# Mixing first in four groups of 512, then the feed-forward in three groups of 704: a hybrid decoder layer on one core

## The chip, the core and the metric

The kernel runs on one core of one Trainium2 chip. The metric is the device time of one execution in microseconds (us), the median of several runs. The engines are named as in the profile: PE (TensorE, matmuls; PEld its weight loads), DVE (VectorE), ACT (ScalarE), POOL (GpSimd), and SP (SyncE), whose queue issues nearly all DMAs.

## The reference

One decoder layer over a prompt of 2048 tokens and a sample of 8 x 8 = 64 tokens that share all weights: model width 1024, feed-forward width 4096. Cut to what matters:

```python
proj = rmsnorm(x, norm_mix_w) @ w_in            # 1024 -> 4096 columns
# 4 retention heads: q, k (rotary), v, gate; 4 HGRN2 heads: q, f, v, gate; all 128 wide
o_r = (head_rmsnorm(chunk_gla(rq, rk, rv, log_gamma)) * silu(rg))
o_h = (head_rmsnorm(chunk_gla(hq, 1 - f, hi, log(f))) * silu(hg))
x = x + concatenate([o_r, o_h]) @ w_out         # 1024 -> 1024, the residual
x = x + square(relu(rmsnorm(x, norm_ffn_w) @ w_up)) @ w_down
y = rmsnorm(x, final_norm_w)                    # for prompt and sample; the final states of the heads are outputs too
```

`chunk_gla` is a causal linear recurrence S_t = diag(g_t) S_(t-1) + k_t^T v_t, o_t = q_t S_t. The prompt starts from zero states, each of the eight samples from its own given state.

## The kernel before

Activations lie transposed, with features on the 128 partitions and tokens along the columns. A float32 product is made by three fp32r matmuls: each operand is cut in a rounded part `hi` and the rest `lo`, and hi·hi, hi·lo and lo·hi are added up in PSUM. A weight unit is 128x1024. It is loaded to a tile `raw`, ACT casts it to `hi` (L277), and DVE or POOL subtracts to make `lo` (`second_part`, L292); that subtraction is called a cut here.

The 2112 tokens go through in three groups: 512 prompt tokens; 64 sample and 768 prompt tokens (832); 768 prompt tokens. A group wider than 512 columns is worked in two pieces of half its width (416, 384), since one PSUM bank holds 512 numbers per partition. Each group runs through everything before the next one begins:

- `mix`: for each of 4 head pairs (one retention, one HGRN2 head) the input projection by `proj` (L352), the values (`values`, L728, always 256 columns), the recurrence in chunks of 128 (`mixer`), and the head norm with its gate (`gate`: L368 Ln, L369 Exp, L1161 multiply).
- `out_proj`: the residual. It stays in SBUF for the feed-forward of that group.
- the feed-forward. Group 0 does it plainly (`ffn_first`: `up_first`, `down_first`). Groups 1 and 2 do it by seven products in place of eight (`ffn`: `up_quad` for the first of eight up sets, `up` for the others, `down` for eight sets in four pairs). A pair of down sets is called an octet: 7 products times 2 sets, 14 weight units of 24 matmuls.

Seven products need sums of weight quarters, S1 to S4, and sums of activation quarters, T1 to T4 (`block_sum`, L1382; the cut of each operand is in `halve`, L1371 and L1375). The weight sums are made once, by DVE, beside the work of groups 0 and 1 (`plan_sums`, L1324), and written to DRAM (`sums`). Groups 1 and 2 read them back like any weight. The products' PSUM results are added by DVE (L1516 in `up`, L1589 in `down`). The hi and lo parts of the input projection's and residual's weights made in group 0 are also written to DRAM and read back by groups 1 and 2 (`kept`, entries "p" of the stream).

The order of the work is set in the code: `plan_stream` lists the weight units in order of use, `weight(i)` loads and prepares units up to two ahead, and side work is put on an agenda (`later(n, fn)`: after n more calls of `tick`, one for each product step). The program of each engine runs in the resulting order. `fetch` (L241) keeps some DMAs of the SP queue in program order.

The lines that cut and choose the engine for a weight:

```python
            if pool or j < 4:
                self.second_part(j, self.nc.gpsimd if pool else self.nc.vector)
            else:
                self.later(4, self.second_part, j, self.nc.vector)
...
        self.stream += [entry(name, ("d", o, v), W_DQ0 + 4 * (2 * o + v), not end and (2 * k + v) % 5 in (1, 3))
                        for v in range(2)]
```

Of the kernel before, what the change touches and what calls it, by code (L numbers as in the profile page):

```python
# [28 lines left out]
SLAB = 832  # L29
NSLAB = 42  # L30
NLD = 6
# [5 lines left out]
GROUPS = ((0, 0, 512), (NS, 512, 768), (0, 1280, 768))  # L37
NT = NS + SEQ
WT = 1024
N_IN, N_OUT, N_UP, N_DN = 32, 8, 32, 32  # L40
W_OUT0 = N_IN
W_UP0 = W_OUT0 + N_OUT
W_DN0 = W_UP0 + N_UP
NQ = FF // (4 * P)
NO = NQ // 2

W_UQ0 = W_DN0 + N_DN
W_DQ0 = W_UQ0 + N_UP
NW = W_DQ0 + N_DN

N_MADE = 4

# [10 lines left out]
PLACE = {name: q for q, name in QUARTER.items()}  # L63
# [17 lines left out]
N_ORDER = (0, 1, 4, 5, 2, 3, 6, 7)  # L81

# [63 lines left out]
def in_blocks():  # L146
    for p in range(H):
        if p:
            yield from ((7, p - 1), (3, p - 1))
        yield from ((5, p), (4, p), (0, p), (1, p), ("v", p))  # L150
    yield from ((7, H - 1), (3, H - 1))


def lay_out_weights(w_in, w_out, w_up, w_down):
    w = np.empty((NW, P, WT), np.float32)
    wi = w_in.reshape(KB, P, 8, H, DK)
    i = 0
    for part, p in in_blocks():
        if part != "v":
            w[i] = wi[:, :, part, p].transpose(1, 0, 2).reshape(P, WT)  # L160
            i += 1
            continue
# [6 lines left out]
    for ps in (range(0, H - 1), range(H - 1, H)):  # L169
        bl = [wo[kind, p, :, n] for n in N_ORDER for p in ps for kind in (1, 0)]  # L170
        for j in range(0, len(bl), 8):
            w[i] = np.stack(bl[j:j + 8], 1).reshape(P, WT)
            i += 1
    wu = w_up.reshape(KB, P, FF // P, P)
    for f in range(FF // P):
        w[i] = wu[:, :, f].transpose(1, 0, 2).reshape(P, WT)
        i += 1
    wd = w_down.reshape(8, 4, P, 4, 256)
    for f in range(8):
        for n in range(4):  # L180
            w[i] = wd[f, :, :, n].transpose(1, 0, 2).reshape(P, WT)
            i += 1
# [25 lines left out]
class Kernel:  # L208
# [12 lines left out]
    def tick(self):  # L221
        self.now += 1
        while self.agenda and self.agenda[0][0] <= self.now:
            _, _, fn, a = heapq.heappop(self.agenda)
            fn(*a)
        self.n_ticks += 1
        while self.side and self.side[0][0] <= self.n_ticks:
            self.side.popleft()[1]()
# [8 lines left out]
    def get(self, dt=F32):  # L237
        return self.sl.tile([P, SLAB], dt, tag="slab", name="slab")
# [6 lines left out]
    def load(self):  # L245
        return self.ld.tile([P, SLAB], F32, tag="ld", name="ld")

# [4 lines left out]
    def weight(self, i):  # L252
        n = len(self.stream)
        while self.w_next < min(i + 1 + self.ahead, n):
            j = self.w_next
            e = self.stream[j]
            if e[0] == "p":

                self.wts[j] = tuple(self.wp.tile([P, WT], F32R, tag=tag, name=tag) for tag in ("hi", "lo"))
                for part, kept in zip(self.wts[j], self.kept[e[1]]):  # L260
                    self.nc.sync.dma_start(part.bitcast(F32), kept)
                self.w_next += 1
                self.w_load = max(self.w_load, j + 1)
                continue
            while self.w_load <= j or j >= self.n_first and self.w_load <= j + 2 and self.w_load < n:
                if self.stream[self.w_load][0] == "p":
                    break
                k, later = self.w_load, self.w_load >= self.n_first
                raw = self.raws[k] = self.wp.tile([P, WT], F32, tag="sum" if later and k % 3 else "raw", name="raw",
                                                  bufs=4 if later and k % 3 else 2)  # L270
                e = self.stream[k]
                self.fetch(raw, self.sums[e[1]] if e[0] == "s" else self.I["w"][e[1]])
                self.w_load += 1
            raw = self.raws.pop(j)
            hi = self.wp.tile([P, WT], F32R, tag="hi", name="hi")
            lo = self.wp.tile([P, WT], F32R, tag="lo", name="lo")
            self.nc.scalar.copy(hi, raw)  # L277
            self.wts[j] = (hi, lo)
            self.second[j] = raw
            pool = len(self.stream[j]) > 2 and self.stream[j][2]  # L280
            if pool or j < 4:
                self.second_part(j, self.nc.gpsimd if pool else self.nc.vector)
            else:
                self.later(4, self.second_part, j, self.nc.vector)
            self.w_next += 1
        self.second_part(i, self.nc.vector)
        return self.wts[i]

    def second_part(self, j, eng):
        if j in self.second:  # L290
            hi, lo = self.wts[j]
            eng.tensor_tensor(out=lo, in0=self.second.pop(j), in1=hi.bitcast(F32), op=ALU.subtract)  # L292

    def plan_stream(self):

        self.stream = [("w", j) for j in range(W_UP0)]
        up = [[("w", W_UP0 + 4 * t + i) for i in range(4)] for t in range(NQ)]
        dn = [[("w", W_DN0 + 4 * t + i) for i in range(4)] for t in range(NQ)]
        self.stream += up[0]
        for t in range(NQ):  # L300
            self.stream += (up[t + 1] if t < NQ - 1 else []) + dn[t]
        self.n_first = len(self.stream)

        def entry(name, key, i0, pool):
            return ("s", key + (name,), pool) if name[0] == "S" else ("w", i0 + A_PLACE[name], pool)

        for g in range(1, len(GROUPS)):
            self.stream += [("p" if j >= N_MADE else "w", j) for j in range(W_UP0)]
            self.stream += [("w", W_UQ0 + i, i % 2) for i in range(4)]
            for t in range(1, NQ):  # L310
                self.stream += [entry(name, ("u", t), W_UQ0 + 4 * t, name in ("A12", "S1", "S4")) for name, _ in PRODUCTS]
            for o in range(NO):
                for k, (name, *_) in enumerate(LAST_OCTET if o == NO - 1 else OCTET):
                    end = g == len(GROUPS) - 1 and o == NO - 1 and k > 4
                    self.stream += [entry(name, ("d", o, v), W_DQ0 + 4 * (2 * o + v), not end and (2 * k + v) % 5 in (1, 3))
                                    for v in range(2)]

    def next_weight(self):
        i = self.w_use
        self.w_use += 1  # L320
        r = self.weight(i)
        if N_MADE <= i < W_UP0:
            self.kept[i] = [self.dp.tile([P, WT], F32, name=f"w{i}{part}") for part in ("hi", "lo")]
            for part, kept in zip(r, self.kept[i]):
                self.nc.sync.dma_start(kept, part.bitcast(F32))
        self.wts.pop(i - 4, None)
        return r

    def take(self, n):

        out = []
        for _ in range(n):
            if not self.blocks:
                hi, lo = self.next_weight()
# [1469 lines left out]
```

## Time and profile before

| | us |
|---|---|
| median of 3 runs (lowest to highest) | 2559.78 (2559.78 to 2560.04) |
| span of the profiled execution | 2557.8 |
| its PE busy / DVE / ACT / POOL | 2527.3 / 1702.4 / 1172.3 / 704.8 |
| DMA moved in it | 443.13 MB, 173 GB/s in the mean |

The profiled execution's own time is taken as its span and the 2.0 us by which the median lies above it. A "busy" engine is one with an instruction in flight; matmuls are pipelined, so the time of one is best read from how many fit in a stretch. In 40 slices the granted TensorE clock reads 9 (nine tenths or more) throughout. By the widths of the matmuls (512, 416 and 384 columns) the three groups take about 630, 1010 and 920 us.

### The profile page before, as it was taken

How to read it: one execution, taken by the hardware profiler on the slowest of the kernel's cores; microseconds unless marked ns; L12 is line 12 of the kernel's file. 1: busy time of each engine (PE TensorE's matmuls, PEld its weight loads, DVE VectorE, ACT ScalarE, POOL GpSimd, SP SyncE). 2: the span in 40 equal slices, each digit the busy share in tenths (PEclk: the TensorE clock that was granted, in tenths of full speed). 3: DMA queues.
4: the chain of work that ended last, by engine and by line, in shares of the span. 5: the costliest groups of instructions: out<-in, count | busy, mean ns of one | idle time of the engine just before them, and what ended most of it. 6: DMA issues, size and time to landing. Idle time of an engine off the chain costs nothing. (4 is left out here: it accounts for less than half of the span.)

```text
span 2557.8 us, 37262 instructions
## 1 busy us (share of the span) xinstructions
PE 2527.3 (99%) x14681; PEld 2398.5 (94%) x14681; DVE 1702.4 (67%) x2165; ACT 1172.3 (46%) x1591; POOL 704.8 (28%) x453
## 2 busy tenths in 40 slices
PE   8999999999999999999999999999999999999997
PEld 7888888888999999999999999999999999999997
DVE  6777775556667667664656978775456465559886
ACT  6776532325444444344434544544445264344443
POOL 4333241111324243101222322243134012223222
PEclk9999999999999999999999999999999999999999
DMA  7666854563264564634457545342223325565552
GB/s 265 219 220 223 294 197 172 190 215 125 94 231 152 198 205 173 230 126 165 166 171 258 191 173 170 129 165 93 94 100 112 120 91 179 176 226 186 176 179 83
DMA packets 147391, 443.13 MB, mean 173 GB/s; under 512 B 15120, under 2 KB 37392, under 8 KB 147216
## 3 DMA queue, kind: packets, MB, share of 16 engines
q1 hardware_dynamic: 147072, 440.73, 49.8%
q8 instruction: 116, 1.90, 0.3%
q14 instruction: 59, 0.48, 0.1%
q10 hardware_dynamic: 144, 0.02, 0.0%
HBM read 331.11 MB, written 108.79 MB: 172 GB/s over the span
## 5 line engine op out<-in xcount | busy, mean ns | idle before, releaser
L352 PE MATMUL pj<-slab,hi 128*128 128x416 f32 (+2 forms) x2844 | 739.3, 363 | 7.4 <-ACT hi L277 6.3
L277 ACT CAST hi<-raw 128x1024 fp32r<-128x1024 f32 x330 | 347.7, 1054 | 673.4 <-PE pu L1176 191.5
L352 PEld LDWEIGHTS pj<-slab,hi 128*128 128x128 f32 x2844 | 513.0, 189 | 38.7 <-ACT hi L277 6.3
L292 POOL TENSOR_TENSOR lo<-raw,hi 128x1024 fp32r<-128x1024 f32 x92 | 248.0, 2695 | 849.6 <-ACT hi L277 788.9
L1176 PE MATMUL pd<-slab,hi 128*128 128x416 f32 (+1 forms) x1792 | 469.4, 342 | 5.1 <-DVE slab L1619 3.1
L292 DVE TENSOR_TENSOR lo<-raw,hi 128x1024 fp32r<-128x1024 f32 x238 | 302.0, 1269 | 199.1 <-ACT hi L277 198.6
L352 PE MATMUL pj<-slab,lo 128*128 128x416 f32 (+2 forms) x1422 | 433.6, 363 | 0.0
L1176 PE MATMUL pu<-slab,hi 128*128 128x416 f32 (+1 forms) x1600 | 408.3, 342 | 0.0
L1176 PEld LDWEIGHTS pd<-slab,hi 128*128 128x128 f32 x1792 | 329.6, 188 | 8.7 <-DVE slab L1619 3.7
L1176 PE MATMUL pd<-slab,lo 128*128 128x416 f32 (+1 forms) x896 | 307.8, 344 | 0.0
L1176 PEld LDWEIGHTS pu<-slab,hi 128*128 128x128 f32 x1600 | 294.0, 188 | 1.5
L352 PEld LDWEIGHTS pj<-slab,lo 128*128 128x128 f32 x1422 | 259.5, 188 | 15.4 <-DVE lo L292 0.8
L1176 PE MATMUL pu<-slab,lo 128*128 128x416 f32 (+1 forms) x800 | 264.2, 343 | 0.0
L352 PE MATMUL mm<-slab,hi 128*128 128x512 f32 x740 | 229.6, 390 | 0.0
L728 PE MATMUL pjv<-hi,slab 128*128 128x256 f32 x1088 | 212.4, 287 | 1.3 <-ACT slab L738 1.3
L1375 DVE TENSOR_TENSOR slab<-slab 128x832 fp32r<-128x832 f32 (+1 forms) x144 | 163.0, 1149 | 36.9 <-ACT slab L1371 17.4
L728 PEld LDWEIGHTS pjv<-hi,slab 128*128 128x128 f32 x1088 | 174.3, 190 | 3.7 <-ACT slab L738 2.2
L1371 ACT CAST slab<-slab 128x832 fp32r<-128x832 f32 (+1 forms) x144 | 122.4, 862 | 116.2 <-DVE slab L1382 83.2
L1176 PEld LDWEIGHTS pd<-slab,lo 128*128 128x128 f32 x896 | 168.1, 188 | 0.5
L352 PEld LDWEIGHTS mm<-slab,hi 128*128 128x128 f32 x740 | 138.5, 188 | 29.2 <-ACT slab L1206 0.4
L728 PE MATMUL pjv<-lo,slab 128*128 128x256 f32 x544 | 153.8, 283 | 0.0
L1176 PEld LDWEIGHTS pu<-slab,lo 128*128 128x128 f32 x800 | 149.7, 188 | 0.5
(214 smaller groups left out, 3685.8 us busy)
## 6 DMA issues: line engine op xcount, KB each, us to landing
raw<-w SPq DMA_DIRECT2D x270, 512.0 KB, 4.2
u<-ld SPq DMA_DIRECT2D x32, 416.0 KB, 4.5
slab<-u SPq DMA_DIRECT2D x32, 416.0 KB, 5.6
u<-ld SPq DMA_DIRECT2D x32, 384.0 KB, 4.5
slab<-u SPq DMA_DIRECT2D x32, 384.0 KB, 5.7
ld<-x SPq DMA_DIRECT2D x16, 416.0 KB, 6.1
ld<-x SPq DMA_DIRECT2D x16, 384.0 KB, 4.1
raw<-su1S SPq DMA_DIRECT2D x8, 512.0 KB, 4.3
```

Source lines behind the costliest of these rows:

```text
L277: self.nc.scalar.copy(hi, raw)
L292: eng.tensor_tensor(out=lo, in0=self.second.pop(j), in1=hi.bitcast(F32), op=ALU.subtract)
L352: self.nc.tensor.matmul(pj[:, i, :T2], w, a[:, c0:c1], start=j == 0 and q == 0, stop=j == n - 1 and q == 2)
L728: nc.tensor.matmul(pj[:, i * 256:(i + 1) * 256], a[:, s:s + C], ww, start=kb == 0 and q == 0, stop=kb == KB - 1 and q == 2)
L1176: self.nc.tensor.matmul(*a, **k)
L1371: self.nc.scalar.copy(hi[:, :g.T], B[name][:, :g.T])
L1375: self.nc.vector.tensor_tensor(out=lo[:, :g.T], in0=B[name][:, :g.T], in1=hi.bitcast(F32)[:, :g.T], op=ALU.subtract)
```

## The change

All groups are mixed first, and all feed-forward comes after, in groups of other sizes.

- **Groups.** Mixing has four groups: three of 512 prompt tokens, one of 64 sample and 512 prompt tokens (576, in two pieces of 288). The feed-forward has three groups of 704 tokens (two pieces of 352), each by seven products. There is no plain feed-forward but for the first up set.
- **Weights in mixing.** The input projection, without values, is in half units (four 128x128 blocks, 128x512). Group 0 cuts them on DVE; groups 1 to 3 load them again, cast on ACT (L345) and cut on POOL (L431, 128x512), 48 per group in place of reading kept parts. Two tiles (`NSUM`) hold the raw halves. Six tiles `w` hold finished parts: a half unit takes one, a full unit two. Kept parts are still read back for the values and the residual's weights.
- **Weight sums.** They are made on POOL in every feeding group (`first_sums`, L397: S1, S2, S3; `last_sum`, L404: S4) from the four raw quarters, which stay in SBUF (16 tiles). Nothing of them is kept in DRAM; `plan_sums` is gone. In the up stage all cuts are on DVE; in the down stage the same 6 of 14 as before are on POOL.
- **Between the phases.** The residual of heads 0 and 1 of each kind is made in the mixing phase (`out_part`) and written with x to DRAM (L1510); the outputs of heads 2 and 3 are written to DRAM (`spill`, L1474) and read back by the feeding groups (`load_heads`, `gather`, L624), which make the other half of the residual. SBUF and PSUM pools are closed after mixing and others opened: four single banks and four more in mixing, four double banks in feeding.
- **x.** The input is read twice for each mixing group after the first: for the sums of squares and to scale it (`norm_squares`, `norm_apply`), with the norm's factor put into the operand.
- **End.** The last norm puts its constant into the Ln's input (`guard`), so two small multiplies fall away.

```diff
-GROUPS = ((0, 0, 512), (NS, 512, 768), (0, 1280, 768))
+GROUPS = ((0, 0, 512), (0, 512, 512), (0, 1024, 512), (NS, 1536, 512))
+NFG = 3
+NRAW, NSUM, NFRAW = 4, 2, 16
...
-            sums = [(("u", t), W_UQ0 + 4 * t) for t in range(1, NQ)]
-            sums += [(("d", o, v), W_DQ0 + 4 * (2 * o + v)) for o in range(NO) for v in range(2)]
-            for i, g in enumerate(gs):
...
-                if i == 0:
-                    self.mix(g)
-                    self.plan_sums(sums[:NQ - 1], [90 + 200 * j for j in range(NQ - 1)])
...
-                    self.out_proj_first(g)
-                    self.ffn_first(g, nxt)
...
-                self.mix(g)
-                self.out_proj(g)
...
-                self.ffn(g, nxt)
+            with ExitStack() as mixing:
+                self.mixing_pools(mixing)
+                self.mix_all(gs)
+            with ExitStack() as feeding:
+                self.feeding_pools(feeding)
+                self.feed_all(gs)
...
+        for i, g in enumerate(gs):
+            self.mix(g, gs[i + 1] if i + 1 < len(gs) else None)
+            self.out_part(g)
...
+        with self.soon():
+            self.load_heads(fs[0], (2, 3))
+            self.flush()
+        for i, g in enumerate(fs):
+            if i:
+                self.finish(fs[i - 1])
+            self.out_proj(g)
+            self.ffn(g, fs[i + 1] if i + 1 < NFG else None)
...
+        elif kind == "raw":
+            self.half_unit(j, self.raws.pop(j), nc.gpsimd)
...
+        if j + 4 in self.sets:
+            self.first_sums(self.sets[j + 4])
...
+    def first_sums(self, key):
+        x, eng = self.parts_of[key], self.nc.gpsimd
+        x["S1"], x["S2"] = self.feed_raw(), self.feed_raw()
+        for out, a, op, b in (("S1", "A21", ALU.add, "A22"), ("S2", "S1", ALU.subtract, "A11"),
+                              ("A21", "A11", ALU.subtract, "A21")):
+            eng.tensor_tensor(out=x[out], in0=x[a], in1=x[b], op=op)
+        x["S3"], x["last"] = x["A21"], (x["A11"], x["A12"], x["S2"])
+
+    def last_sum(self, key):
+        x = self.parts_of[key]
+        if "last" in x:
+            x["S4"], a, b = x.pop("last")
+            self.nc.gpsimd.tensor_tensor(out=x["S4"], in0=a, in1=b, op=ALU.subtract)
```

How the engines' programs read now, at the places that the prediction speaks of. First POOL in the down stage (L292 before and L431 now are cuts, L397 and L404 weight sums). Before, from the last group's gates to its end:

```order
L863 TENSOR_TENSOR slab<-slab 128x96x4
L864 TENSOR_TENSOR slab<-slab 128x96x4
L863 TENSOR_TENSOR slab<-slab 128x192x2
L864 TENSOR_TENSOR slab<-slab 128x192x2
L1027 TENSOR_TENSOR slab<-slab 128x768
L1035 TENSOR_TENSOR slab<-slab 128x768
L292 TENSOR_TENSOR lo<-raw,hi 128x1024 x45
L1656 TENSOR_TENSOR slab<-slab 128x768 x3
```

Now, where the down stage of a feeding group begins:

```order
L397 TENSOR_TENSOR raw<-raw 128x1024 x3
L404 TENSOR_TENSOR raw<-raw 128x1024
L431 TENSOR_TENSOR w<-raw,w 128x1024
L404 TENSOR_TENSOR raw<-raw 128x1024
L431 TENSOR_TENSOR w<-raw,w 128x1024 x2
L397 TENSOR_TENSOR raw<-raw 128x1024 x3
L431 TENSOR_TENSOR w<-raw,w 128x1024
L397 TENSOR_TENSOR raw<-raw 128x1024 x3
L431 TENSOR_TENSOR w<-raw,w 128x1024 x2
L404 TENSOR_TENSOR raw<-raw 128x1024
```

Where 45 cuts stood by themselves, each pair of sets now brings eight sums among its six cuts.

Second, PE at the last gates of a group, whose column sums before are L505 and L506 (the L352 rows around them are the residual's matmuls):

```order
L352 MATMUL pj<-slab,hi 128x384 x2
L505 MATMUL mm<-slab,ones_r 128x384
L506 MATMUL mm<-slab,ones_r 128x384
L352 MATMUL pj<-slab,hi 128x384 x2
L352 MATMUL pj<-slab,lo 128x384 x2
L352 MATMUL pj<-slab,hi 128x384 x4
L352 MATMUL pj<-slab,lo 128x384 x2
L505 MATMUL mm<-slab,ones_r 128x384
L506 MATMUL mm<-slab,ones_r 128x384
```

Now, at the end of mixing (L663 and L664 are the column sums, L1494 first the residual's part and then, 352 wide, the first residual of the feeding phase):

```order
L1494 MATMUL pj<-slab,w 128x288 x2
L1383 MATMUL mm<-slab 128x128 x2
L1494 MATMUL pj<-slab,w 128x288
L663 MATMUL mm<-slab,ones_r 128x320
L664 MATMUL mm<-slab,ones_r 128x320
L663 MATMUL mm<-slab,ones_r 128x256 x2
L664 MATMUL mm<-slab,ones_r 128x256 x2
L1494 MATMUL pj<-slab,w 128x352 x812
```

The last column sums are followed at once by matmuls that need the heads' outputs; nothing stands between. On the SP queue the same place reads now (o are the heads' outputs in DRAM, r the partial residuals):

```order
L1474 DMA o_12791<-slab 128x576
L1474 DMA o_12793<-slab 128x576
L364 DMA w<-w38lo 128x1024
L624 DMA slab<-o_2500 128x512
L624 DMA slab<-o_5390 128x192
L624 DMA ld<-r_2792 128x512
L624 DMA ld<-r_5668 128x192
L308 DMA raw<-w 128x1024
L624 DMA slab<-o_2498 128x512
```

The loads of the first feeding group stand behind the stores of the last heads.

Third, SP at the start, before:

```order
L241 DMA slab<-x 128x512
L241 DMA raw<-w 128x1024
L241 DMA slab<-x 128x512 x7
L241 DMA raw<-w 128x1024 x2
L241 DMA ld<-cs 128x512 x2
```

and now:

```order
L234 DMA slab<-x 128x512
L234 DMA raw<-w 128x1024 x4
L234 DMA slab<-x 128x512
L234 DMA ld<-x 128x512 x4
L234 DMA slab<-x 128x512
L302 DMA raw<-w 128x512 x2
L234 DMA slab<-x 128x512 x5
```

Between the first and the last of the eight x blocks there were one raw weight, and are now four, two halves and four blocks of the next group's x.

More of the change, by code (lines that the diff above doesn't have):

```diff
@@ L245, in load @@
     def load(self):
-        return self.ld.tile([P, SLAB], F32, tag="ld", name="ld")
+        return self.ld.tile([P, self.slab], F32, tag=self.tags[1], name="ld")
     def getr(self):
         return self.get(F32R)
[L252 to L285, printed above, removed]
@@ L289, in second_part, with quarter @@
+    def quarter(self, bp, i, name, j):
+        x = self.pair_sums_of(bp, i)
+        if name == "S4":
+            self.second_part(j - 2, self.nc.vector)
+            self.nc.gpsimd.tensor_tensor(out=x["S4"], in0=x["A12"], in1=x["S2"], op=ALU.subtract)
+        return x[name]
     def second_part(self, j, eng):
         if j in self.second:
[L291 to L316, printed above, removed]
@@ L1345, in out_proj @@
+            pj = self.proj(g, self.take(4), acts)
+            for ps, c0, c1 in pj:
+                with self.soon():
+                    self.nc.vector.tensor_tensor(out=x[:, c0:c1], in0=ps, in1=x[:, c0:c1], op=ALU.add)
+            g.part[n] = self.dp.tile([P, g.T], F32, name=f"r{g.i}{n}")
+            self.nc.sync.dma_start(g.part[n], x[:, :g.T])
     def out_proj(self, g):
         nc, T2 = self.nc, g.T // 2
-        part = self.residual(g)
-        acts = g.oc[H - 1]
+        acts = [a for p in (2, 3) for a in g.oc[p]]
```

1046 lines of the change are left out of this document (608 added, 438 removed).

## The prediction

> **What bounds the kernel now.** I read the head of the page first, for the engines' shares, then the waits, to see who stops TensorE (PE).
>
> ```profile
> span 2557.8 us, 37262 instructions
> PE 2527.3 (99%) x14681; PEld 2398.5 (94%) x14681; DVE 1702.4 (67%) x2165; ACT 1172.3 (46%) x1591; POOL 704.8 (28%) x453
> ...
> PE pj L352 <- ACT hi L277: 6.3, 1, 6.3
> ...
> PE pd L1176 <- DVE slab L1619: 3.1, 2, 2.1
> ...
> PE pd L1176 <- DVE slab L1589: 2.0, 3, 1.3
> ```
>
> PE is busy 2527.3 of 2557.8 us: matmuls set the time, and the 30.5 us left are a start of 6.3, gaps of about 2 us, and a tail. So the change gains what it takes off PE's stream, and loses whatever makes PE wait where now it doesn't. Next come stretches of one stage each. The columns are: stretch, its length, then busy time and instructions of PE, PE's weight loads, DVE, ACT and POOL, the granted clock, the DMA share and GB/s.
>
> ```profile
> 4.00:8.00 4.00, 1.67 (x3) 0.95 (x4) 3.39 (x10) 3.35 (x6) 0.00 (x0) 1.00 1.01 360
> 8.00:12.00 4.00, 4.00 (x12) 3.07 (x12) 4.00 (x7) 3.98 (x7) 0.00 (x0) 1.00 1.04 392
> 64.00:128.00 64.00, 63.98 (x395) 55.30 (x394) 47.74 (x92) 45.25 (x73) 20.55 (x21) 1.00 0.63 220
> 500.00:564.00 64.00, 64.00 (x284) 53.01 (x283) 37.45 (x37) 20.57 (x26) 12.67 (x8) 1.00 0.55 195
> 1216.00:1280.00 64.00, 64.00 (x341) 63.39 (x340) 41.90 (x38) 25.60 (x28) 15.04 (x6) 1.00 0.49 166
> ...
> 2112.00:2176.00 64.00, 64.00 (x371) 64.00 (x370) 36.09 (x36) 31.39 (x36) 17.11 (x7) 1.00 0.58 185
> ...
> 2304.00:2368.00 64.00, 62.80 (x361) 61.99 (x359) 60.55 (x56) 31.39 (x36) 19.43 (x6) 1.00 0.53 183
> 2531.00:2558.00 27.00, 12.55 (x62) 10.17 (x60) 16.62 (x25) 10.32 (x20) 8.05 (x7) 0.86 0.32 117
> ```
>
> The rows with PE at 64.00 price a matmul: 64/284 = 0.2254 us at 512 columns (plain feed-forward of group 0), 64/341 = 0.1877 at 416 (group 1), 64/371 = 0.1725 at 384 (group 2). The exception matters most: 2304 to 2368, the first eighth of group 2's down projection, has DVE at 60.55 beside POOL at 19.43, and there PE lost 1.2. The timeline of DVE and POOL shows how those two get along (start, duration, engine, line):
>
> ```profile
> 2298.11 1.21 DVE L292 TENSOR_TENSOR lo<-raw,hi 128x1024 fp32r<-128x1024 f32 x1
> ...
> 2300.11 0.95 DVE L1382 TENSOR_TENSOR slab<-slab 128x768 f32<-128x768 f32 x1
> 2300.98 0.95 DVE L1516 TENSOR_TENSOR ld<-pu,slab 128x768 f32<-128x768 f32 x1
> 2301.85 2.36 DVE L1382 TENSOR_TENSOR slab<-slab 128x768 f32<-128x768 f32 x1
> ```
>
> ```profile
> 2300.98 2.41 POOL L292 TENSOR_TENSOR lo<-raw,hi 128x1024 fp32r<-128x1024 f32 x1 [5.34 <-ACT hi L277]
> ...
> 2322.22 5.56 POOL L292 TENSOR_TENSOR lo<-raw,hi 128x1024 fp32r<-128x1024 f32 x1 [10.67 <-ACT hi L277]
> ```
>
> While POOL held 2300.98 to 2303.39, the DVE operation with one input in PSUM (L1516) took its usual 0.95, but the next, with two SBUF inputs (L1382), took 2.36 instead of 0.95 and ended 0.82 after POOL did. POOL's own cut, 2.41 alone, took 5.56 where DVE was dense. So DVE operations with two SBUF inputs and POOL operations take turns; about 0.13 of each (0.95 − 0.82) overlaps at a handover. I call the sum of both kinds the turn load.
>
> **The matmul stream.** Per piece of tokens a group has 576 matmuls of input projection (without values), 192 of residual, 1536 of plain feed-forward, or 1356 by seven products (the first up set stays plain). Before: 2304 at 512 columns, and 2 × 2124 = 4248 each at 416 and 384. After: 3 × 672 = 2016 at 512 and 1344 at 288 in mixing (half of the residual's there), 3 × 2 × (96 + 1356) = 8712 at 352 in feeding. The values' 256-column matmuls stay at 1632. By interpolation 352 columns cost 0.1594 (from 384 and 416, slope 0.0152 for 32), and 288 cost 0.1331 (between 256 and 384, the former at 0.120 from the first and last of 43 value matmuls in a row:)
>
> ```profile
> 33.66 0.40 PE L728 MATMUL pjv<-hi,slab 128*128 128x256 f32 x2
> ...
> 38.70 0.40 PE L728 MATMUL pjv<-hi,slab 128*128 128x256 f32 x2
> ```
>
> Before: 519.3 + 797.3 + 732.8 = 2049.4. After: 454.4 + 1388.7 + 178.9 = 2022.0. That is −27.4; 17 fewer transposes, at no more than that 0.120, give up to −2.0: **−29**. (The Trainium skill, TensorE: Matmul & The Clock Gate, section Back-to-back issue gap, gives N/2.4 + 2.5 ns for a warm matmul, 216 ns at 512, where this trace has 225; by its rule the stream term would be an estimated −35, because more but narrower matmuls then carry less overhead each.)
>
> **The down octets.** The seven products of two quarter pairs (14 weight units, 24 matmuls each) last 14 × 24 × 0.1594 = 53.6 us of PE at 352 columns. DVE cuts 8 of the units and POOL 6, as before. What is new is that POOL makes the eight weight sums of each set again (L397, L404), which before came back from DRAM: 14 POOL operations of 128x1024 an octet instead of 6. The rows for DVE's widths:
>
> ```profile
> L1589 DVE TENSOR_TENSOR slab<-pd,slab 128x768 f32<-128x768 f32 x54 | 51.2, 951 | 20.3 <-PE pd L1176 20.2
> ...
> L1268 DVE TENSOR_TENSOR slab<-mm,slab 128x512 f32<-128x512 f32 x47 | 32.3, 687 | 35.2 <-PE mm L352 35.1
> ```
>
> Between them 704 columns cost 0.885. Turn load: POOL 14 × 2.4 = 33.6; DVE 8 × 1.21 + 22 × 0.885 (14 cuts and 8 sums of activations) = 29.2; together 62.8 against 53.6, so +9.2. The 14 DVE operations that read PSUM may lie beside POOL. Before, the same count at 768 columns was 14.5 + 30.6 = 45.1 against 58.0, which fits: room, except in the first octet, where old work was left over. Nine octets (three in each group; the fourth prepares no next set, so 19.2 + 29.2 fits) give 9 × 9.2 = 83. At most three units prepared ahead (3 × 24 × 0.1594 = 11.5 us) cover part, once in each group: 83 − 34.5 = **+48**. Lower end 0: if 0.13 of each of 44 operations overlaps, the load is 57.1, the excess 3.5 an octet, 10.5 a group, and the units ahead cover it. Upper end: nothing beside anything, 62.8 + 14 × 0.885 = 75.2, hence 9 × 21.6 = 194. I take the whole durations, because L1382 above lost nearly its whole wait. In the up sets four sums and seven DVE cuts a set cost about 20 of 26.8 us: nothing, covered by that room.
>
> (The Trainium skill, SBUF — State Buffer, section Who interferes with whom, says that the pair of ports which DVE and GpSimd share is held for the whole instruction while the other blocks fully, and that DVE with one SBUF input stays out of it. The rows above agree except for the short overlap. By that rule alone, with no overlap and no credit for units ahead, the octets would cost an estimated +83 and the time would be about 2645.)
>
> **Mixing.** In groups 1 to 3 the in-projection's hi/lo halves are no longer read back but cut: 12 POOL operations of 128x512 a head, against a head's 67 us or so.
>
> ```profile
> L696 POOL TENSOR_TENSOR slab<-slab 128x512 f32<-128x512 f32 x4 | 5.3, 1313 | 22.2 <-ACT slab L372 22.2
> ...
> raw<-w SPq DMA_DIRECT2D x270, 512.0 KB, 4.2
> ```
>
> 12 × 1.31 = 15.8 more on POOL's 20.55 in 64: it fits in the mean. Only two raw halves are held: landing (up to 4.2), an ACT cast (0.66, by 4.64/7 in the rows of the start below) and the cut (1.31) make 6.2 for two in turn, 3.1 a half, while PE uses one in 12 × 0.2254 = 2.70. Five halves ahead, 13.5 us, cover that in all but the longest bursts. **+8**, from −6 (the gaps of now gone) to +36 (3 us in each of 12 heads).
>
> **Start.** SP's queue now issues four raw weights (2 MB), four further x blocks and two raw halves ahead of the last five x; the last x lands after 5.5 MB instead of 2.5. At the 360 to 392 GB/s of the first windows that is 8 us later. Now ACT's scaling sets that pace:
>
> ```profile
> 1.63 3.29 SPq L241 DMA_DIRECT2D slab<-x  x7
> 6.14 4.64 ACT L542 ACTIVATE slab<-slab,vec 128x512 fp32r<-128x512 f32 x7
> ...
> 8.14 1.05 PE L352 MATMUL pj<-slab,hi 128*128 128x512 f32 x2
> 9.42 1.05 PE L352 MATMUL pj<-slab,hi 128*128 128x512 f32 x2
> ```
>
> PE advances there by 1.28 for three matmuls that cost 3 × 0.2254 = 0.68 later, so part of the delay replaces slack: **+6** (4 to 8).
>
> **From mixing to feeding.** Before, a group's last gate lay under the residual's matmuls. Now the last two heads' outputs are gated after all mixing matmuls, go to DRAM, and the first residual needs them back. On SP's queue both stores wait for DVE's last gate, and behind them stand head loads among raw weights. The chain for two heads: Ln and Exp, DVE (0.4, by the 0.687 at 512 columns), about 5.4 MB at 370 GB/s = 15 (issues of 0.47 each, 3.29/7 above, run under it), a cast (0.66 × 704/512 = 0.9).
>
> ```profile
> L368 ACT ACTIVATE slab<-mm,eps 128x256 f32<-128x256 f32 x16 | 7.6, 476 | 10.5 <-PE mm L506 10.2 <-DVE S L1082 0.3
> ...
> L369 ACT ACTIVATE slab<-slab 128x256 f32<-128x256 f32 x16 | 6.7, 420 | 0.5
> ```
>
> 2 × 0.9 + 0.4 + 15 + 0.9 = 18, **+18**; the lower end, 10, is when loads go out before the gate ends, the upper, 25, adds the stores' own landing. The tail loses two multiplies: **−1** (PE is idle 14.5 of the last 27).
>
> **Sum.** The profiled execution's span is 2557.8; the runs' median, 2559.78, stands 2.0 above. 2557.8 − 29 + 6 + 18 + 8 + 48 − 1 = 2607.8, plus 2.0: **2610**.
>
> **Rivals.** *Faster:* the units ahead and the handover overlaps hide the octets' turn load entirely, the mixing term is 0, loads run ahead at the transition (10) and the start costs 4: 2557.8 − 29 + 4 + 10 − 1 + 2 = 2544. For it: at 2304 to 2368 DVE was at 60.55 and PE lost only 1.2. Against it: POOL had 6 cuts there, not 14. It decides if the octets cost under some 11 us. *Same:* the octets are hidden, start, mixing and transition are paid in full: −29 + 6 + 18 + 8 − 1 = +2, 2562. *Heavier:* DVE's queue is in order, so an operation that waits for POOL holds those that read PSUM behind it; POOL issues three sums in a row (7.2 us, by the 5.56 row some 13) ahead of a cut that PE needs within 11.5. Halfway to the upper end, (48 + 194)/2 = 121: 2683. For it: the 5.56; against it: PE's loss of 1.2 now.
>
> **How the numbers follow.** What a measurement of this kernel can tell from no change is 0.2%, 5.1 us: 2554.7 to 2564.9. My forecast, octets partly stalled, 2580 to 2640: 0.45. Heavier, above 2640: 0.14. Octets hidden but the rest paid, 2555 to 2580: 0.16, of which 0.10 is within 0.2%. Faster, 2530 to 2554: 0.25. The range of 8 in 10 leaves a tenth at each end: 2540 to 2665; the forecast's own is 2580 to 2640. Faster 0.25, same 0.10, slower 0.65.
>
> **What would show it.** The waits of PE on the cuts and sums of the down stage (L431, L397, L404), with DVE and POOL operations stretched beyond 1.21 and 2.41 in three octets of each group; a gap of 10 to 25 at about 45% of the span; feeding stretches with 401 matmuls in 64 us where nothing waits. If PE stands at 64.00 through the down octets, the turn-load term is wrong, and the time falls to 2544 to 2562. If 352 columns cost other than 0.1594, 8712 of them move the sum by 8.7 us for each ns.

## The result: 9.2% slower, and the profile after

The changed kernel takes 2795.93 us (median of 4 runs, 2794.47 to 2799.46) against 2559.88: a ratio of 1.0924, 95% interval 1.0908 to 1.0939. The prediction said slower, 2610, and up to 2665: the sign was right, the size far too small. The head of the page, and the waits of PE:

```profile
span 2793.2 us, 41519 instructions
PE 2580.1 (92%) x15998; PEld 2441.8 (87%) x15998; DVE 2109.7 (76%) x2549; ACT 1338.1 (48%) x2114; POOL 1296.3 (46%) x790
...
PE pj L1494 <- DVE slab L1758: 62.2, 15, 6.8
PE pj L1494 <- ACT slab L1538: 31.5, 6, 6.7
PE mm L663 <- ACT slab L479: 15.6, 8, 6.3
```

PE's idle time rose from 30.5 to 213 us, and its busy time rose too, by 53, where the stream should have saved 29: the 82 us between the two are matmuls at a slow clock, as the table below shows. By stages it looks as follows (stretch, length, busy time and instructions of PE, PEld, DVE, ACT, POOL, granted clock, DMA share, GB/s):

```profile
0.00:100.00 100.00, 75.00 (x362) 60.03 (x363) 69.09 (x108) 55.76 (x92) 34.60 (x39) 0.86 0.44 160
100.00:1100.00 1000.00, 961.40 (x6274) 856.31 (x6273) 637.27 (x1202) 573.16 (x1108) 500.42 (x465) 0.99 0.44 142
1100.00:1263.90 163.90, 145.78 (x998) 141.44 (x997) 90.11 (x167) 66.05 (x125) 36.05 (x32) 0.94 0.58 199
1263.90:1461.20 197.30, 196.16 (x1235) 195.87 (x1234) 161.98 (x126) 92.26 (x108) 91.99 (x32) 1.00 0.43 141
1461.20:1732.80 271.60, 230.42 (x1314) 226.97 (x1313) 241.71 (x180) 93.45 (x109) 151.75 (x53) 0.91 0.35 115
...
1990.80:2259.40 268.60, 229.44 (x1314) 226.25 (x1313) 242.40 (x180) 93.47 (x109) 152.72 (x53) 0.91 0.35 117
...
2519.60:2771.90 252.30, 219.73 (x1269) 216.79 (x1268) 233.69 (x180) 95.12 (x114) 136.93 (x48) 0.92 0.23 79
```

The fourth row is an up stage, where next to nothing waits (196.16/1235 = 0.159 us a matmul, as priced). The last three are the down stages of the three feeding groups: 792 us for 3897 matmuls that were priced at 621, with DVE at nine tenths, and a clock of 0.91. For comparison before, the same windows of the start, two mixing stretches and the last down stage:

```profile
0.00:40.00 40.00, 32.52 (x157) 26.68 (x158) 24.60 (x39) 29.65 (x40) 15.21 (x19) 1.00 0.79 281
40.00:100.00 60.00, 58.71 (x361) 49.91 (x360) 45.05 (x86) 40.83 (x67) 20.75 (x22) 1.00 0.68 232
100.00:330.00 230.00, 228.69 (x1308) 194.39 (x1307) 170.74 (x288) 142.52 (x234) 83.87 (x75) 1.00 0.68 236
...
626.00:1100.00 474.00, 469.86 (x3077) 454.81 (x3076) 319.63 (x491) 195.70 (x299) 146.62 (x118) 1.00 0.53 180
...
2300.00:2531.00 231.00, 228.99 (x1318) 227.91 (x1317) 194.53 (x182) 104.44 (x118) 66.47 (x26) 1.00 0.46 161
```

What a stage loses is PE's idle time plus what a slow clock adds to its busy time (busy x (1 - clock)). After less before:

| term | predicted | measured | of that, slow clock |
|---|---|---|---|
| matmul stream | -29 | -29 (by its prices, which hold) | |
| start, 0 to 100 | +6 | 35.5 - 8.8 = +27 | 10 |
| mixing, 100 to about 1150 | +8 | about +44 | 7 |
| transition, about 1150 to 1264 | +18 | about +20 | 6 |
| down octets | +48 | 172 - 2 = +170 | 59 |
| rest of feeding, tail | -1 | +6 - 3 = +3 | |
| sum | +50 | +235 (measured: +235.4) | 82 |

That the sum comes out so close is partly luck: the clock has two digits (for mixing it is taken in windows of 50 to 250 us), and busy x (1 - clock) also counts slow clock that falls in a wait. Cut where each 336th matmul of the down stage begins, the four octets of the first group are:

```profile
1455.00:1525.10 70.10, 60.03 (x338) 58.94 (x337) 68.25 (x51) 29.12 (x35) 40.69 (x15) 0.90 0.39 133
1525.10:1596.60 71.50, 59.92 (x338) 58.86 (x337) 68.03 (x51) 25.06 (x30) 42.49 (x15) 0.88 0.30 100
1596.60:1666.20 69.60, 59.21 (x337) 58.44 (x336) 65.49 (x48) 25.88 (x30) 39.67 (x15) 0.93 0.34 113
1666.20:1731.60 65.40, 56.24 (x339) 55.73 (x338) 45.24 (x36) 17.39 (x19) 33.83 (x13) 0.95 0.33 106
```

The first three last about 70 us where 53.6 were priced, and DVE is busy nearly throughout. How a stall in a down stage looks, first DVE, then POOL, then PE (start, duration; in brackets the idle time before, and what ended it):

```profile
1499.48 2.29 DVE L1542 TENSOR_TENSOR slab<-slab 128x704 fp32r<-128x704 f32 x1
1501.70 3.36 DVE L431 TENSOR_TENSOR w<-raw,w 128x1024 fp32r<-128x1024 f32 x1
1504.98 0.88 DVE L1542 TENSOR_TENSOR slab<-slab 128x704 fp32r<-128x704 f32 x1
1505.79 0.88 DVE L1758 TENSOR_TENSOR slab<-pj,slab 128x704 f32<-128x704 f32 x1
```

```profile
1498.03 2.99 POOL L397 TENSOR_TENSOR raw<-raw 128x1024 f32<-128x1024 f32 x1 [1.16 <-DVE w L431]
1500.98 3.00 POOL L431 TENSOR_TENSOR w<-raw,w 128x1024 fp32r<-128x1024 f32 x1
```

```profile
1506.81 23.40 PE L1494 MATMUL pj<-slab,w 128*128 128x352 f32 x127 [4.98 <-DVE slab L1758]
```

DVE's cuts of 0.88 and 1.21 take 2.29 and 3.36 while POOL runs a sum and a cut. The addition L1758, which empties the PSUM banks that PE wants next, reads PSUM and takes its usual 0.88, but it stands behind them in DVE's queue, and PE waits 4.98 for it. Of the 113 us that PE idles in the three down stages, 62 end with L1758, 32 with ACT's casts of activation sums (L1538, which wait for DVE's sums, L1549), 15 with ACT's casts of weights (L351) and 4 with DVE's cuts. The groups of the whole run say the same: L1758 keeps its 0.88, the operations on SBUF are stretched.

```profile
L431 DVE TENSOR_TENSOR w<-raw,w 128x1024 fp32r<-128x1024 f32 x273 | 438.1, 1607 | 43.0 <-ACT w L351 37.6 <-PE pj L1494 2.2
L397 POOL TENSOR_TENSOR raw<-raw 128x1024 f32<-128x1024 f32 x135 | 397.9, 2956 | 162.7 <-DVE w L431 109.3 <-DMA raw<-w 48.0
L1542 DVE TENSOR_TENSOR slab<-slab 128x704 fp32r<-128x704 f32 x216 | 314.7, 1477 | 34.9 <-ACT slab L1538 28.6 <-PE pj L1494 5.0
...
L1758 DVE TENSOR_TENSOR slab<-pj,slab 128x704 f32<-128x704 f32 x166 | 145.7, 881 | 57.8 <-PE pj L1494 57.8
```

### The profile page after: what moved, and what is told of

Its sections match the earlier page's. It is cut to its first block, busy times and chain, and to the rows that moved or that the text cites. A ratio compares the mean times of both kernels' runs of the same rounds, so it can differ in the third digit from the quotient of the medians.

```text
span 2793.2 us, 41519 instructions
## 1 busy us (share of the span) xinstructions
PE 2580.1 (92%) x15998; PEld 2441.8 (87%) x15998; DVE 2109.7 (76%) x2549; ACT 1338.1 (48%) x2114; POOL 1296.3 (46%) x790
## 5 line engine op out<-in xcount | busy, mean ns | idle before, releaser
L1494 PE MATMUL pj<-slab,w 128*128 128x352 f32 (+2 forms) x12072 | 2189.8, 339 | 143.0 <-DVE slab L1758 62.2
L1494 PEld LDWEIGHTS pj<-slab,w 128*128 128x128 f32 x12072 | 1991.9, 193 | 228.0 <-ACT slab L1538 71.4
L351 ACT CAST w<-raw 128x1024 fp32r<-128x1024 f32 x343 | 359.7, 1049 | 538.4 <-PE pj L1494 510.7
L431 POOL TENSOR_TENSOR w<-raw,w 128x512 fp32r<-128x512 f32 (+1 forms) x212 | 395.2, 1870 | 458.1 <-ACT w L351 213.0
L431 DVE TENSOR_TENSOR w<-raw,w 128x1024 fp32r<-128x1024 f32 (+1 forms) x323 | 477.0, 1482 | 55.2 <-ACT w L351 37.6
L397 POOL TENSOR_TENSOR raw<-raw 128x1024 f32<-128x1024 f32 x135 | 397.9, 2956 | 162.7 <-DVE w L431 109.3
L1542 DVE TENSOR_TENSOR slab<-slab 128x704 fp32r<-128x704 f32 x216 | 314.7, 1477 | 34.9 <-ACT slab L1538 28.6
L404 POOL TENSOR_TENSOR raw<-raw 128x1024 f32<-128x1024 f32 x45 | 127.0, 2822 | 424.4 <-DVE w L431 423.4
L1538 ACT CAST slab<-slab 128x704 fp32r<-128x704 f32 x216 | 163.1, 778 | 275.3 <-DVE slab L1549 202.3
L1494 PE MATMUL pj<-w,slab 128*128 128x256 f32 x1632 | 232.1, 291 | 12.2 <-DVE slab L1012 9.3
L1494 PEld LDWEIGHTS pj<-w,slab 128*128 128x128 f32 x1632 | 211.0, 195 | 15.8 <-ACT slab L788 6.5
L1758 DVE TENSOR_TENSOR slab<-pj,slab 128x704 f32<-128x704 f32 x166 | 145.7, 881 | 57.8 <-PE pj L1494 57.8
L1549 DVE TENSOR_TENSOR slab<-slab 128x704 f32<-128x704 f32 x120 | 179.2, 1509 | 1.4 <-PE pj L1494 1.2
L345 ACT CAST w<-raw 128x512 fp32r<-128x512 f32 x192 | 116.3, 618 | 80.9 <-DMA raw<-w 46.0
```

The source lines that it names most:

```text
L345: self.nc.scalar.copy(t[:, :HALF], raw)
L397: eng.tensor_tensor(out=x[out], in0=x[a], in1=x[b], op=op)
L404: self.nc.gpsimd.tensor_tensor(out=x["S4"], in0=a, in1=b, op=ALU.subtract)
L431: eng.tensor_tensor(out=lo, in0=raw, in1=hi.bitcast(F32), op=ALU.subtract)
L1494: self.nc.tensor.matmul(out, w, a, **k)
L1538: self.nc.scalar.copy(hi[:, :g.T], B[name][:, :g.T])
```

## Experiments

Each label was run once beside the kernel before unless runs are named; the changed kernel's four runs lie 5 us apart, so differences under some 8 us between single runs decide nothing by themselves.

### What stalls the down stage

**Without the sums** (`e1_no_sums`), 2673.96:

```diff
+        if key[1] == "d":
+            x["S1"], x["S2"], x["S3"], x["S4"] = x["A21"], x["A22"], x["A11"], x["A12"]
+            return
         x["S1"], x["S2"] = self.feed_raw(), self.feed_raw()
```

> Leaves out the weight sums of the down sets: S1 to S4 are the raw quarters A21, A22, A11, A12 (so the down projection computes something else); all cuts and products stay. Theory T (DVE operations with two SBUF inputs and POOL operations take turns, and DVE's queue is in order, so the additions that read PSUM stand in the same row): an octet then has POOL 6 x 2.4 = 14.4, DVE 29.2 + 12.4 = 41.6, less 0.13 for each of 36 handovers, 51.3 us, under PE's 53.6; the three down stages (271, 268, 252 us) fall to about 214 each, the granted clock there goes from 0.91 to 1.00, time about 2647 (2630 to 2665). Rival R1 (narrow pieces of 352 columns and four double banks make PE wait for banks whatever POOL does): 2780 to 2796. Rival R2 (raw quarters land late): no change either, and ACT's casts wait for DMA.

**Sums on DVE** (`e2_sums_dve`), 2722.95: `first_sums` and `last_sum` use `nc.vector` for keys "d".

> The eight sums of an octet go from POOL to DVE (1.21 each instead of 2.4), cuts stay. T: 14.4 + 41.6 + 8 x 1.21 = 65.7, less 0.13 x 44 = 60.0 an octet in three octets of each group, against some 69 now: about 25 us less a group, time about 2715 (2690 to 2735). R1: no change. Rival R3 (DVE alone is the bound, POOL does not matter): DVE has 9.7 more an octet, so slower than now by up to 9 x 9.7 = 87.

**Sums and cuts on DVE** (`e3_all_dve`), 2676.72: as before, and

```diff
-... name, not end and (2 * k + v) % 5 in (1, 3)) for v in range(2)]
+... name, False) for v in range(2)]
```

> Sums and all cuts of the down stage on DVE, POOL has nothing there. T: nothing takes turns; DVE 22 x 1.21 + 36 x 0.885 = 58.5 an octet by whole durations, about 54 by the spacing of operations back to back (each starts 0.08 before the one before it ends), against PE's 53.6: down stages 216 to 235 each, time 2650 to 2700, faster than with the sums alone on DVE. R3: slower than with the sums alone on DVE by 9 x 6 x 1.21 = 65. R1: no change.

**Memsets in place of the sums** (`e11_memset`), 2664.92:

```diff
-            eng.tensor_tensor(out=x[out], in0=x[a], in1=x[b], op=op)
+            if key[1] == "d":
+                for _ in range(3):
+                    eng.memset(x[out], 0.5)
+            else:
+                eng.tensor_tensor(out=x[out], in0=x[a], in1=x[b], op=op)
```

The same is done in `last_sum`.

> The changed kernel itself, but each of the down sets' weight sums on POOL is replaced by three memsets of the same tile (about 0.93 each, 2.8 together, by the memsets of 128x384 and 128x576; they write and read nothing), so the down projection computes something else. POOL is as busy as with the sums and DVE's work is the same. Theory T in the form that two readers of SBUF take turns (as the Trainium skill has it: SBUF — State Buffer, section Who interferes with whom: a DVE instruction with two SBUF inputs contends with a GpSimd instruction that reads, not with one that only writes): as with the sums left out, 2665 to 2690. Rival R4 (any POOL instruction blocks DVE): about 2796. Rival R5 (PE waits because POOL itself comes late with the cuts and sums, whatever DVE does): also near 2780 to 2796.

The first group's down stage in these four, in the order of the text:

```profile
1459.90:1692.30 232.40, 218.11 (x1336) 217.01 (x1335) 195.06 (x180) 96.12 (x112) 81.30 (x29) 0.97 0.39 126
```

```profile
1469.90:1712.10 242.20, 221.58 (x1335) 218.03 (x1334) 224.12 (x205) 95.59 (x112) 87.90 (x29) 0.96 0.38 129
```

```profile
1459.30:1693.50 234.20, 219.30 (x1341) 217.62 (x1341) 220.67 (x229) 95.85 (x112) 16.49 (x6) 0.97 0.40 132
```

```profile
1466.40:1693.60 227.20, 218.62 (x1336) 217.59 (x1335) 193.41 (x180) 96.49 (x112) 142.28 (x99) 0.98 0.42 138
```

And the memsets among POOL's groups in the last:

```profile
L399 POOL MEMSET raw<- 128x1024 f32 x216 | 205.7, 956 | 166.4 <-DMA raw<-w 124.0 <-DVE w L439 33.4
```

From 271.6 the stage falls to 232.4 without the sums, to 242.2 with the sums on DVE, and to 234.2 with everything on DVE, although DVE then has the most operations (x229 instead of x180) and, by whole durations, more work than the octet is long. DVE's own work does not make the stall (R3), nor do narrow pieces or banks (R1) or late raw quarters (R2), by which e1 would have changed nothing. The memsets are the sharpest: POOL is nearly as busy as with the sums (142.28 against 151.75) and writes three times as much, DVE is as busy as without the sums (193.41 against 195.06), and the stall is gone (227.2). So neither POOL's time nor its instructions as such hold DVE up (R4, R5), but POOL's reading of SBUF. This is as the Trainium skill has it (SBUF — State Buffer, section Who interferes with whom): a DVE instruction with two SBUF inputs contends with a GpSimd instruction that reads SBUF, not with one that only writes it.

### What is left in feeding

**No POOL cuts or sums anywhere** (`e5_no_pool`), 2638.03: e3 and e4 (below), and `nc.vector` in `first_sums` and `last_sum` throughout.

> All weight cuts and all weight sums of both phases on DVE: the edits of e3_all_dve and e4_mix_dve, and also the up sets' sums. With all cuts and sums of the down stage on DVE, groups 1 and 2 still lose some 20 us in the last octet of the down stage, where POOL makes the next group's first up sums (PE gaps of 6.1 and 7.0). Theory T (every POOL operation beside dense DVE work costs): these go too, 2677 - 16 - 25 = 2636 (2625 to 2650). Rival R3 (DVE is the bound by its own work): the up stage now has 11 x 1.21 + 9 x 0.885 = 21.3 of 26.8 us a set on DVE and the last octets no less, so no gain beyond the 16: 2655 to 2675.

**Sums from DRAM** (`e8_sums_dram`), 2624.76: the first feeding group stores each sum, and groups 1 and 2 load each unit by itself:

```diff
+        elif e[0] == "x" and e[1][0]:
+            ...
+            src = self.sums[key[1:] + (name,)] if name[0] == "S" else self.I["w"][base + A_PLACE[name]]
+            self.nc.sync.dma_start(self.raws[j], src)
```

> As e5_no_pool, but the first feeding group writes its weight sums to DRAM and groups 1 and 2 read them back, each weight unit loaded by itself. T: DVE in groups 1 and 2 falls to 14 x 1.21 + 36 x 0.885 = 48.8 an octet, under 53.6: their down stages end at 212 to 216 us, 10 to 25 less in all than e5_no_pool. If PE's matmuls already set the pace there: within 5 us.

The first group's down stage of the one, and the second group's of the other:

```profile
1444.30:1667.60 223.30, 218.35 (x1341) 216.46 (x1341) 216.08 (x234) 95.86 (x112) 0.00 (x0) 0.99 0.40 138
```

```profile
1921.40:2137.30 215.90, 215.90 (x1342) 215.90 (x1341) 186.24 (x203) 96.11 (x112) 0.00 (x0) 1.00 0.60 199
```

Both came out as theory T had them. In the last row PE has no idle time at all: this stage is bound by matmuls again, at 215.9 where 214 were priced. The last octet of the first group shows where the time went, in e3 and then in e5:

```profile
1620.20:1692.30 72.10, 58.16 (x338) 57.34 (x337) 59.80 (x57) 23.75 (x29) 16.49 (x6) 0.91 0.32 107
```

```profile
1605.60:1666.40 60.80, 56.61 (x339) 55.58 (x337) 54.89 (x61) 23.71 (x29) 0.00 (x0) 0.97 0.36 118
```

The three octets before it last 54.1 to 54.6 us in both runs. So to take POOL's first up sums of the next group from it gained some 11 us in the last octet; some 7 of the excess stay in e5, and in e8's second group, where DVE has less to do, all four octets last 54.1. The same last octet, 64.1 us in e1, is part of why e1 ended 9 us above its range; its second and third octets, 57.8 and 58.7, lost some 4 us each as well.

### Mixing

**Cuts on DVE** (`e4_mix_dve`), 2779.94: `nc.vector` for units of kind "raw".

> The raw halves of mixing groups 1 to 3 are cut on DVE (0.69) instead of POOL (1.31 to 1.37); feeding as it is. If the cuts on POOL cause the mixing gaps (PE idle 42 us from 100 to 1150): 20 to 35 us less, 2765 to 2780. If they come from chains of the mixer and of the norms at the groups' beginnings: within 8 us of 2796, or slower since DVE gets 48 x 0.69 = 33 us more a group.

**Kept halves** (`e6_kept`), 2638.97 against 2638.03 of e5: every half unit of group 0 is stored, and is of kind "op" in groups 1 to 3.

> As e5_no_pool, but the half units of the input projection are kept in DRAM by group 0 and read back by groups 1 to 3 (no cast, no cut, no raw halves there), as the kernel before did with whole units. If preparing weights is what still makes PE wait in mixing: 10 to 25 us less than e5_no_pool. If the waits are the mixer's and the norms' own chains, which a group of 512 covers less than one of 768 to 832: within 6 us of e5_no_pool.

**A later cast of reloaded heads** (`e15_late_cast`), 2603.12 against 2615.89 of e9 (below):

```diff
-        self.cut(s, hi, lo, g.T, 2)
+        self.later(14, self.cut, s, hi, lo, g.T, 2)
```

> As e9_start_rt, but a reloaded head is cast 14 ticks (about 4 us) after its load is issued instead of at once in ACT's program. If the mixing gaps come from ACT standing in its queue for that DMA (ACT waits 25.9 us for it between 100 and 1100, and PE 9.7 us for the operations behind it): 8 to 15 us less than e9_start_rt, 2601 to 2608. If the gaps are the gates' and mixer's own chains: within 3 us of 2616.

The time fell by 16 us, under the 20 expected, and only some 12 of it lie in mixing: the up stage begins at 1252.0 instead of 1263.9. How the halves are prepared beyond that costs nothing that shows (e6). ACT's queue does: in e9, between 100 and 1100, ACT stood for reloaded heads, and PE for what was behind them (ACT's waits, then PE's):

```profile
ACT slab L493 <- DMA slab<-o: 25.9, 13, 3.9
```

```profile
PE mm L677 <- ACT slab L493: 9.7, 5, 6.2
```

With the later cast both rows are gone, and the time falls by 12.8. Some 25 us of PE's idle time in mixing stay; that they are the heads' own chains, which a group of 512 covers less than one of 832, was only argued.

### Start

**Order of the loads** (`e7_start`), 2642.95 against 2638.03 of e5: `self.ordered = False` moves behind group 0, and raw halves are loaded by `fetch`.

> As e5_no_pool, but in group 0 the loads of later x blocks and raw halves stay behind the first eight x blocks and the first weights on the SP queue. By the start term (+6, of which 1.5 MB of 3 MB falls away): 3 to 5 us less than e5_no_pool. By the rival, that the start lost its time later (PE idle 17 us between 40 and 100, where DVE scales and cuts eight blocks of x that PE's first value matmuls need): under 3 us, since the later wait absorbs it.

**First values from unscaled x** (`e9_start_rt`), 2615.89 against 2624.76 of e8: `values` of the first head pair runs before `g.h` becomes the scaled x, and its results are scaled per token.

```diff
+                                nc.scalar.activation(v[:, cc], pj[i // 2][:, cc], AF.Copy,
+                                                     scale=rt[:, i0 + i - 1 + k:i0 + i + k])
```

> As e8_sums_dram, but the first head pair's values in group 0 are made from the unscaled x and scaled per token when they leave PSUM (as the kernel before did for all), so that PE does not wait there for DVE to scale and cut eight blocks. If that wait is the start's loss (PE idle 12.2 in three gaps between 46 and 60, and a granted clock of 0.77 from 40 to 100): 12 to 22 us less than e8_sums_dram, 2603 to 2613. If the wait only moves on to the mixer's chain of the first head: 0 to 6 us less.

From 40 to 100 in the changed kernel, and in e9:

```profile
40.00:100.00 60.00, 42.55 (x238) 36.68 (x239) 49.83 (x74) 34.95 (x58) 27.86 (x24) 0.77 0.34 118
```

```profile
40.00:100.00 60.00, 50.55 (x296) 43.57 (x296) 51.24 (x87) 41.48 (x69) 31.81 (x26) 0.91 0.44 153
```

The loads' order was no loss that shows: PE reached the first value matmuls 1.3 us earlier and had lost it again by the end. The wait for the scaled x was a part: without it two of the three gaps (2.9 and 3.2) are gone and PE does 58 more matmuls in the stretch, yet only 9 us of it reach the end, between the two ranges expected. The first gap, 6.1 us from 46.15, stays in e9: PE waits there for a DVE operation behind others with two SBUF inputs, while POOL is busy throughout. Whether the two take turns there as in the down stage was not tested.

### Transition

**The last store from POOL's queue** (`e10_spill_pool`), 2626.65 against 2624.76 of e8; **the first feeding group's loads from POOL's queue** (`e13_heads_pool`), 2658.95 (4 runs, 2653.54 to 2665.24; ratio to the kernel before 1.0396, 1.0376 to 1.0416); **the heads' loads from ACT's queue** (`e14_heads_act`), 2622.87; the last two against 2615.89 of e9.

```diff
-            self.nc.sync.dma_start(dst[:, to], tiles(m)[:, at])
+            q = self.nc.gpsimd if self.feeding and g.i == 0 else self.nc.sync
+            q.dma_start(dst[:, to], tiles(m)[:, at])
```

> As e8_sums_dram, but the last mixing group's outputs of the last head pair go to DRAM from POOL's queue instead of SP's, so that the loads of the first feeding group do not stand behind them. If SP's order makes the gap at the transition (PE idle 9.3 there, the loads are issued 0.8 after the two stores): 3 to 8 us less. If the loads wait for memory that the last mixing operations hold: within 2 us.

> As e9_start_rt, but the first feeding group's loads of heads and partial residuals are issued from POOL's queue, so that on SP's queue nothing stands ahead of them (there a kept weight waits for a tile that PE's last residual part still reads). If that order holds them up: the PE gap at the transition, 9.3 us, falls to 2 to 5, and with the clock that falls in it 5 to 10 us less than e9_start_rt, 2606 to 2611. If the memory for the loaded heads comes free only with the last mixing operations: within 2 us of 2616. Slower than the kernel before in both cases, since the mixing phase still leaves PE idle some 29 us between 100 and 1100.

> As e9_start_rt, but the heads of the first feeding group are loaded from ACT's queue (with POOL's queue the first arrived early, PE began the first residual 14 us earlier, and then each further transfer took POOL 2.5 to 8 us to issue). If SP's order makes the transition's gap: PE idle there 9.3 falls to 1 to 5, 4 to 10 us less than e9_start_rt, 2606 to 2612. If the memory for the later heads comes free only at the end of mixing: within 2 us of 2616.

None shortened the gap of about 9 us (in e14 it came as four gaps of 6.8, 3.9, 2.6 and 1.7, since loads and casts stood in one queue; e14 missed both of its ranges, by less than single runs can differ). The POOL queue missed by far, and in a way that tells something; its DMA issues, with the idle time before each, in the timeline of POOL:

```profile
1173.03 0.55 POOL L639 DMA_DIRECT2D ld<-r  x1 [4.05 <-issue]
1181.16 0.54 POOL L639 DMA_DIRECT2D ld<-r  x1 [7.58 <-issue]
1188.09 0.55 POOL L639 DMA_DIRECT2D ld<-r  x1 [6.39 <-issue]
```

POOL issues a transfer only every 2.5 to 8 us, where SP takes 0.3 to 0.6, and PE waited 25 us for the second head. Whether SP's order or the memory decides the gap stays open.

**Both** (`e16_both`), 2597.43 (4 runs, 2595.70 to 2603.46; ratio 1.0155, 1.0138 to 1.0172): e14 and e15 together.

> Both edits, of the loads from ACT's queue and of the later cast. If both mechanisms hold: 2592 to 2604; if only one: 2601 to 2612; if none: 2614 to 2618. The kernel before stays faster in each case, by 1.3 to 2.3%.

It has the lowest median of this design's versions, and the kernel before stays 1.5% faster. The single run of e15, 2603.12, lies within its four, so that the loads from ACT's queue add anything to the later cast is not shown.

## Why the prediction was right and wrong

- **The stream** held: 0.159 us at 352 columns where nothing waits, against the interpolated 0.1594. The prediction's bracket names the wrong pair for it: 0.1594 lies between the prices at 256 and 384 columns, while the slope of 0.0152 from 384 and 416 would have given 0.1573 and a stream term of about -47.
- **The octets** were the step that failed: +48 predicted, +170 measured. That operations take turns was right, and e11 shows it. The size failed in three places.
  - The turn load (62.8 us) left out the 14 DVE operations that read PSUM, because they "may lie beside POOL". They lose no time to POOL (L1758 keeps its 0.88), but they stand in order among those that do, and PE waits for them. The upper end, 75.2 an octet, was the model to take: less 0.13 for each of 44 handovers it gives 69.5, and the first three octets of the three groups last 69.5 to 71.5, with DVE busy 65 to 68 of them. Against the 54.1 us of an octet that waits for nothing (e8), these nine lose 146 us.
  - The credit of 34.5 us for units prepared ahead did not appear: the first octet of each group, which they should have shortened, lasts 69.7 to 70.1, as long as the others.
  - The fourth octet was not free: it lasts 65.4, 63.0 and 58.1 us, 24 more in all. In the first two groups POOL makes the next group's first up sums there.

  The slow clock, 59 us of the 170, needs no term of its own in the octets: DVE's queue sets their length, and with DVE busy 68 of 70 us faster matmuls would mostly have waited longer. That is an inference from these rows; no run separates the two.
- **The rival that I called heavier**, with DVE's queue in order, is what happened; I gave it 0.14 against 0.45, because PE lost only 1.2 in the window from 2304 to 2368 before. That window had 6 POOL operations an octet, and the row did not bear on 14. The row of 5.56 spoke for it. Even its price, 2683, was 113 too low.
- **Mixing**, +8 for about +44: the term priced only POOL's cuts (some 12 by e4) and had none for heads that are stored and read back in ACT's queue (13 by e15), nor for the clock. The rest, some 20, stays open.
- **Start**, +6 for +27: the term was for a late x, and that cost next to nothing. By 40 us PE had done 124 matmuls of 512 columns, 27.9 us by their price; before it was 98 of these and 55 value matmuls of 256 columns, 28.7. The loss lies between 40 and 100 and had no term: gaps of 6.1, 2.9 and 3.2 where PE waits for DVE, partly for x scaled and cut, which the change puts ahead of the first values, and the slow clock after them (0.77).
- **Transition**, +18 for about +20, is partly luck: the gap that the chain of stores and loads leaves is 8.9 us (10 to 25 predicted); smaller gaps and the slow clock, some 6 each, make up the rest. The **tail**, -1 for -3, went the way it was worked out.

## What to carry to other kernels

- Where two engines take turns at SBUF, add up the whole queue of the in-order one, the operations that take no turn too, if anything that PE waits for stands among them. A load over PE's time then means a stall in every period; lookahead doesn't help for long.
- To move two-input SBUF work from DVE to POOL in a stage where DVE is dense makes both slower: here the down sets' sums took 2.8 to 3.0 us each on POOL and 1.35 to 1.5 on DVE (e2), and the kernel was 73 us faster with them on DVE. Writing without reading (memsets) cost DVE nothing in e11.
- Where PE's own stream sets the pace, a sum of waits needs a term for the slow matmuls after each wait: the gaps of 3.3 us and more in the down stages were followed by a loss of about half of themselves. Where another engine's queue sets the pace, that loss is inside the queue's time.

## What the runs showed of the hardware

The granted clock after the stall of 4.98 us at 1501.8 to 1506.8 (2 us a row, columns as above):

```profile
1499.00:1501.00 2.00, 2.00 (x14) 2.00 (x13) 2.00 (x2) 0.43 (x1) 2.00 (x2) 1.00 0.00 0
...
1507.00:1509.00 2.00, 2.00 (x7) 2.00 (x8) 2.00 (x4) 0.00 (x0) 0.00 (x0) 0.50 0.98 378
1509.00:1511.00 2.00, 2.00 (x8) 2.00 (x8) 2.00 (x4) 0.78 (x1) 0.00 (x0) 0.50 0.97 362
1511.00:1513.00 2.00, 2.00 (x9) 2.00 (x9) 0.80 (x2) 0.00 (x0) 0.00 (x0) 0.56 0.59 154
1513.00:1515.00 2.00, 2.00 (x14) 2.00 (x13) 1.35 (x2) 1.46 (x2) 0.32 (x1) 1.00 0.42 172
```

From 1507 on PE is busy in all of them, and does half the matmuls for about 5.5 us. In the three down stages PE has 24 gaps of 2 us or more, 109 us in all. After 23 of them, 3.29 to 6.77 us long, matmuls came 0.29 us apart instead of 0.16, for 3.4 to 6 us; after the one of 2.62 us, at 1702.18, the clock stayed at 1.00. The slow stretches, 4.7 us in the mean, cost half of that, 23 x 2.3 = 54 us; the 59 of the table also counts clock that falls in the waits (0.91 over the 4.98 us of this one). The Trainium skill (TensorE: Matmul & The Clock Gate, Part 1: The HAM clock gate) has the half clock after an idle window of about 3.4 us and its end after as long a busy one. The trace agrees in the half and about in the length of the gap, for the shortest that led to it in these stages has 3.29 us; the slow clock often lasted longer than one such window.
